# The low halves of the weights: a subtraction on the vector engine, or a negated copy plus an adding DMA

## The chip, the cores and the metric

The kernel runs on one core of a Trainium2 chip. The core has a matrix engine (PE, TensorE; its weight loads are listed apart as PEld), a vector engine (DVE), a scalar engine (ACT), GpSimd (POOL) and a queue engine (SP). POOL and SP here mostly issue DMAs. Each engine runs its own instructions strictly in order and waits on semaphores for the others. The metric is the device time of one execution in microseconds.

## The reference

The reference is a two-layer encoder trunk on 512 tokens of width 1024, all in float32:

```python
for l in range(DEPTH):                       # DEPTH = 2
    x = x + 0.5 * swiglu_ffn(rmsnorm(x, ffn1_norm[l]), ffn1_w_up[l], ffn1_w_down[l])
    x = x + mixer(rmsnorm(x, mix_norm[l]), ...)
    x = x + 0.5 * swiglu_ffn(rmsnorm(x, ffn2_norm[l]), ffn2_w_up[l], ffn2_w_down[l])
    x = rmsnorm(x, final_norm[l])
```

The mixer projects to q, k, v, a gated convolution input and two gates. It runs banded attention in three dilation groups (window 128, 512, 2048 at dilation 1, 4, 16), a depthwise convolution of width 31 with layer norm, combines the two branches by the gates and projects back. The hidden width of the feed-forward part (FFN) is 2816.

## The kernel before

Every weight matrix is read from DRAM once, in pieces of up to 128 x 1024 float32 (512 KB). A matmul here takes operands in the reduced format float32r, so each float32 operand is split in two: an upper half `hi` (the value rounded to float32r) and a lower half `lo` (what is left). `mm3` (L156) then makes three matmuls per product: hi by hi, hi by lo, lo by hi.

The function `stage` (L140) makes one such piece ready. SP loads it into `raw` (2 buffers), ACT copies it, rounding, into `hi` (L152), and DVE subtracts `hi` from `raw` into `lo` (L153). `hi` and `lo` have 4 buffers each, so PE works on one piece while up to three others are made ready. There are 448 pieces. `stage` is called with a priority 150 steps ahead of its place in the program; the order on each engine is set by a scheduler that runs when the program is built.

Who calls it:
- `ffn`: the up projection, 4 pieces for each of 11 pairs of hidden tiles, and the down projection through `proj_cols`. One full piece feeds 24 matmuls of 128x128 by 512 columns.
- `mixer`, in `proj_cols`: the convolution input (`ps_ga`, `ps_gg`), the gates (`ps_gc`, `ps_gA`), and the projections `ps_cp`, `ps_ap`, `ps_o`.
- `mixer`, in `tokens_chunk` (L295): q, k and v, nine chunks per layer. A chunk takes four pieces and goes through all four twice (two token tiles each time, `ps_n`), so that in the second pass a piece feeds 12 matmuls and its buffers come free one after another near the end of the chunk.

In the mixer POOL issues small DMAs: `bias` (L302, two buffers), v tiles to DRAM and back in another order (`vd` L380, `V` L390 to L395), attention results (`od` L463, `sd` L466 to L471) and their return (`oin` L572, `sa` L540). Some of them wait for DVE, ACT or PE. DVE meanwhile runs the convolution (`cv`, L516, 240 instructions per layer) between everything else.

In the last two groups of each down projection and of the output projection (28 pieces in all) the rows are 128 elements (512 bytes) long instead of 256.

Of the kernel before, what the change touches and what calls it, by code (L numbers as in the profile page):

```python
# [11 lines left out]
F32 = mybir.dt.float32  # L12
F32R = mybir.dt.float32r
AF = mybir.ActivationFunctionType
ALU = mybir.AluOpType
# [29 lines left out]
def trunk(ctx: ExitStack, tc: tile.TileContext, A: dict, out: bass.AP):  # L45
    nc = tc.nc
# [89 lines left out]
    def uniq(s):  # L136
        cnt[0] += 1
        return f"{s}_{cnt[0]}"

    def stage(*srcs):  # L140

        a, n1 = srcs[0].shape[1], srcs[0].shape[2]
        n = n1 * len(srcs)
        raw = wp.tile([P, 1024], F32, tag="raw", name=uniq("raw"), bufs=2)
        hi = wp.tile([P, 1024], F32R, tag="hi", name=uniq("hi"))
        lo = wp.tile([P, 1024], F32R, tag="lo", name=uniq("lo"))
        m = a * n
        with tc.high_priority(offset=150):
            rv = raw[:, :m].rearrange("p (a n) -> p a n", a=a)
            for i, src in enumerate(srcs):  # L150
                nc.sync.dma_start(rv[:, :, i * n1:(i + 1) * n1], src)
            nc.scalar.activation(hi[:, :m], raw[:, :m], AF.Copy)  # L152
            nc.vector.tensor_sub(lo[:, :m], raw[:, :m], hi[:, :m].bitcast(F32))  # L153
        return (hi[:, :m].rearrange("p (a n) -> p a n", a=a), lo[:, :m].rearrange("p (a n) -> p a n", a=a))

    def mm3(ps, ah, al, bh, bl, first, last):  # L156
# [61 lines left out]
    def proj_cols(src, c0, rhs, nk, ps):  # L218

        nj = len(ps)  # L220
        step = 8 // nj
        for kk in range(0, nk, step):
            n_ = min(step, nk - kk)
            wh, wl = stage(src[:, kk:kk + n_, c0:c0 + nj * P])
            for j in range(nj):
                for k in range(n_):
                    kg = kk + k
                    mm3(ps[j], wh[:, k, j * P:(j + 1) * P], wl[:, k, j * P:(j + 1) * P], *rhs[kg], kg == 0, kg == nk - 1)


    def ffn(l, w_up, w_down, xg, R, after, deferred=None):
        wu = w_up[l].rearrange("(k p) n -> p k n", p=P)
        wd = w_down[l].rearrange("(k p) n -> p k n", p=P)
        with tc.tile_pool(name=uniq("ffn"), bufs=4) as fp:
            h = []
            for m in range(0, NF, 2):
                pss = {}
                for ab in range(2):
                    pss[ab] = [ps_mm(uniq("ps_a")) if ab == 0 else ps_at(uniq("ps_b")) for _ in range(2)]
                    for kk in range(0, KD, 4):  # L240
                        wh, wl = stage(wu[:, kk:kk + 4, ab * FF + m * P:ab * FF + m * P + 256])
                        for j in range(2):
                            for k in range(4):
                                kg = kk + k
                                mm3(pss[ab][j], wh[:, k, j * P:(j + 1) * P], wl[:, k, j * P:(j + 1) * P], *xg[kg], kg == 0, kg == KD - 1)
                for j in range(2):
                    t = fp.tile([P, S], F32, tag="tmp", name=uniq("t"), bufs=7)
                    nc.vector.tensor_mul(t, pss[0][j], R)
                    nc.scalar.activation(t, t, AF.Silu)
                    nc.vector.tensor_mul(t, pss[1][j], t)  # L250
                    h.append(split(fp, t, "h", 2 * NF))
                if m == 0 and deferred is not None:
                    deferred()
            for ts in ((0, 1), (2, 3), (4, 5), (6,), (7,)):
                pss = [(ps_at if ts[0] in (0, 4, 7) else ps_mm)(uniq("ps_d")) for _ in ts]
                proj_cols(wd, ts[0] * P, h, NF, pss)
                for k, ps in zip(ts, pss):
                    t = fp.tile([P, S], F32, tag="tmp", name=uniq("t"), bufs=7)
                    nc.vector.scalar_tensor_tensor(t, ps, 0.5, R, op0=ALU.mult, op1=ALU.mult)
                    nc.vector.tensor_add(xs[k], xs[k], t)  # L260
                    after(k, fp)


    def mixer(l, xg, R, rr, after):
# [5 lines left out]
        with ExitStack() as mx:  # L270
# [26 lines left out]
            def tokens_chunk(cols):  # L297

                n = S // len(cols)
                bias = mp.tile([P, S], F32, tag="bias", name=uniq("bias"), bufs=2)  # L300
                for i, c0 in enumerate(cols):
                    nc.gpsimd.dma_start(bias[:, i * n:(i + 1) * n], bass.AP(tensor=A["b_in"].tensor, offset=A["b_in"].offset + l * IN_W + c0, ap=[[0, P], [1, n]]))  # L302
                w = [stage(*(win[:, kk:kk + 2, c0:c0 + n] for c0 in cols)) for kk in range(0, KD, 2)]
                for t2 in range(0, TT, 2):
                    ps = [ps_mm(uniq("ps_n")) for _ in range(2)]
                    for k in range(KD):
                        wh, wl = w[k // 2][0][:, k % 2], w[k // 2][1][:, k % 2]
                        xh, xl = xg[k]
                        for t in range(2):
                            ts = slice((t2 + t) * P, (t2 + t + 1) * P)  # L310
                            mm3(ps[t], xh[:, ts], xl[:, ts], wh, wl, k == 0, k == KD - 1)
                    for t in range(2):
                        yield t2 + t, ps[t], bias
# [440 lines left out]
```

## Time and profile before

| | |
|---|---|
| median of 3 runs | 2670.15 us (2669.97 to 2671.66) |
| profiled execution | 2669.43 us, of which the span 2667.5 us |
| PE busy | 2617.8 us, 98% of the span |
| DVE busy | 1599.7 us, 60% |
| ACT busy | 1005.8 us, 38% |
| POOL busy | 110.5 us, 4% |
| mean granted clock of PE | 0.992 |
| moved by DMA | 268.65 MB, mean 101 GB/s |

Busy times are sums of instructions, and a share of the span is an average over stages that differ: DVE is at 60% over all, but full in the attention stages. Matmuls overlap each other, so the time from start to start of two matmuls says more than the length of one.

### The profile page before, as it was taken

What the parts mean: (1) busy time and instruction counts of PE and PEld (TensorE: products, weight loads), DVE (VectorE), ACT (ScalarE), POOL (GpSimd) and SP (SyncE); (2) the same over time, 40 slices, a digit from 0 to 9 for tenths busy, and PEclk for the clock granted to TensorE, in tenths of its full rate; (3) what the DMA queues carried; (4) which work ended last, traced back from release to release, by engine and by line L of the source; (5) the groups of instructions that cost most, each with busy time, mean ns of one, the idle gap of its engine ahead of it and who ended that gap; (6) DMA issues with size and microseconds to landing.
All of it is one profiled execution on the core that took longest, in us unless ns stands there. A gap on an engine that the chain in (4) does not pass through costs nothing.

```text
span 2667.5 us, 30985 instructions
## 1 busy us (share of the span) xinstructions
PE 2617.8 (98%) x12125; PEld 2125.9 (80%) x12125; DVE 1599.7 (60%) x2606; ACT 1005.8 (38%) x1572; POOL 110.5 (4%) x208
## 2 busy tenths in 40 slices
PE   8999999998999999999999999999989999999998
PEld 6888888776877788888888888887767778888887
DVE  4444349999985754443454433599999756444432
ACT  5332232233578242232332322322344963322222
POOL 1000000011011000000000000000011110000000
PEclk9999999999999999999999999999989999999999
DMA  4332333233333333332333322323323343333322
GB/s 155 98 95 91 103 99 105 79 113 97 100 112 110 117 95 96 102 95 95 95 95 95 100 94 93 108 91 114 96 85 121 100 126 103 95 95 96 102 91 75
DMA packets 253778, 268.65 MB, mean 101 GB/s; under 512 B 11624, under 2 KB 238320, under 8 KB 253632
## 3 DMA queue, kind: packets, MB, share of 16 engines
q1 hardware_dynamic: 242112, 234.91, 28.3%
q0 software_dynamic: 11504, 31.76, 4.0%
q8 instruction: 95, 1.56, 0.2%
q14 instruction: 51, 0.42, 0.1%
q10 hardware_dynamic: 16, 0.00, 0.0%
HBM read 251.75 MB, written 14.88 MB: 100 GB/s over the span
## 4 chain that ended last, share of the span: by engine, by line
PE 88%; DVE 7%; ACT 3%; issue 1%; DMA 0%; SPq 0%; ACTq 0%
PE ps_a L158 6%; PE ps_a L159 6%; PE ps_b L157 6%; PE ps_d L157 6%; PE ps_b L158 6%; PE ps_b L159 6%; PE ps_d L159 6%; PE ps_d L158 6%; PE ps_a L157 6%; PE ps_n L158 4%; PE ps_n L157 4%; PE ps_n L159 3%; DVE cv L516 2%; PE ps_cp L158 1%; PE ps_cp L159 1%; PE ps_cp L157 1%
## 5 line engine op out<-in xcount | busy, mean ns | idle before, releaser
L153 DVE TENSOR_TENSOR lo<-raw,hi 128x1024 fp32r<-128x1024 f32 (+1 forms) x448 | 539.2, 1204 | 725.0 <-ACT hi L152 724.0
L152 ACT ACTIVATE hi<-raw 128x1024 fp32r<-128x1024 f32 (+1 forms) x448 | 468.1, 1045 | 1058.3 <-issue 360.2
L516 DVE SCALAR_TENSOR_TENSOR cv<-u,cwc,cv 128x500 f32<-128x500 f32 (+14 forms) x480 | 335.7, 737 | 0.1
L158 PE MATMUL ps_b<-xgl,hi 128*128 128x512 f32 x704 | 275.1, 391 | 0.0
L157 PE MATMUL ps_a<-xgh,hi 128*128 128x512 f32 x704 | 273.5, 389 | 1.1 <-ACT xgh L174 1.1
L159 PE MATMUL ps_a<-xgh,lo 128*128 128x512 f32 x704 | 274.5, 390 | 0.0
L158 PE MATMUL ps_a<-xgl,hi 128*128 128x512 f32 x704 | 274.3, 390 | 0.1
L157 PE MATMUL ps_b<-xgh,hi 128*128 128x512 f32 x704 | 274.0, 389 | 0.0
L159 PE MATMUL ps_b<-xgh,lo 128*128 128x512 f32 x704 | 273.9, 389 | 0.0
L159 PE MATMUL ps_d<-sh,lo 128*128 128x512 f32 x704 | 273.9, 389 | 0.0
L157 PE MATMUL ps_d<-sh,hi 128*128 128x512 f32 x704 | 273.9, 389 | 0.0
L158 PE MATMUL ps_d<-sl,hi 128*128 128x512 f32 x704 | 273.9, 389 | 0.0
L158 PE MATMUL ps_n<-lo,xgh 128*128 128x512 f32 x576 | 228.7, 397 | 3.9 <-DVE lo L153 3.8
L159 PE MATMUL ps_n<-hi,xgl 128*128 128x512 f32 x576 | 225.7, 392 | 0.0
L157 PE MATMUL ps_n<-hi,xgh 128*128 128x512 f32 x576 | 215.8, 395 | 4.7 <-DVE tmp L379 3.4
L157 PEld LDWEIGHTS ps_a<-xgh,hi 128*128 128x128 f32 x704 | 132.0, 188 | 29.0 <-ACT xgh L174 1.5
L158 PEld LDWEIGHTS ps_b<-xgl,hi 128*128 128x128 f32 x704 | 132.2, 188 | 28.0 <-issue 0.7
L159 PEld LDWEIGHTS ps_b<-xgh,lo 128*128 128x128 f32 x704 | 132.2, 188 | 28.0 <-issue 0.7
L158 PEld LDWEIGHTS ps_a<-xgl,hi 128*128 128x128 f32 x704 | 132.2, 188 | 27.9 <-DVE xgl L175 0.5
L159 PEld LDWEIGHTS ps_d<-sh,lo 128*128 128x128 f32 x704 | 132.2, 188 | 27.5
L159 PEld LDWEIGHTS ps_a<-xgh,lo 128*128 128x128 f32 x704 | 132.2, 188 | 27.5 <-issue 0.2
L157 PEld LDWEIGHTS ps_b<-xgh,hi 128*128 128x128 f32 x704 | 132.2, 188 | 27.4
(234 smaller groups left out, 3988.1 us busy)
## 6 DMA issues: line engine op xcount, KB each, us to landing
raw<-in_ffn_w_up_dram SPq DMA_DIRECT2D x176, 512.0 KB, 3.5
raw<-in_w_in_dram SPq DMA_DIRECT2D x88, 512.0 KB, 3.6
raw<-in_ffn_w_down_dram SPq DMA_DIRECT2D x76, 512.0 KB, 3.5
raw<-in_w_in_dram SPq DMA_DIRECT2D x96, 256.0 KB, 3.1
raw<-in_w_conv_proj_dram SPq DMA_DIRECT2D x16, 512.0 KB, 3.5
raw<-in_w_out_dram SPq DMA_DIRECT2D x16, 512.0 KB, 3.5
vd<-tmp POOLq DMA_DIRECT2D x24, 256.0 KB, 2.3
od<-ot POOLq DMA_DIRECT2D x24, 256.0 KB, 3.0
```

Source lines behind the costliest of these rows:

```text
L152: nc.scalar.activation(hi[:, :m], raw[:, :m], AF.Copy)
L153: nc.vector.tensor_sub(lo[:, :m], raw[:, :m], hi[:, :m].bitcast(F32))
L157: nc.tensor.matmul(ps, ah, bh, start=first, stop=False)
L158: nc.tensor.matmul(ps, ah, bl, start=False, stop=False)
L159: nc.tensor.matmul(ps, al, bh, start=False, stop=last)
L516: nc.vector.scalar_tensor_tensor(a[:, t0:t1], u[k][:, t0 + d:t1 + d], cw(l, j, k), a[:, t0:t1], op0=ALU.mult, op1=ALU.add)
```

## The change

`stage` no longer calls DVE. ACT makes `hi` as before and then writes `-hi` into `lo`; POOL issues a DMA that reads the same weights once more from DRAM and adds them to `lo` in place. Each weight is now read from DRAM twice, once into `raw` and once into `lo`. `raw` is read by one instruction (ACT's copy) instead of two. All 448 pieces take the new way; no call names another.

```diff
-    def stage(*srcs):
+    def stage(*srcs, rest="dma"):
...
             nc.scalar.activation(hi[:, :m], raw[:, :m], AF.Copy)
-            nc.vector.tensor_sub(lo[:, :m], raw[:, :m], hi[:, :m].bitcast(F32))
+            if rest == "dma":
+
+                nc.scalar.activation(lo[:, :m], hi[:, :m].bitcast(F32), AF.Copy, scale=-1.0)
+                lv = lo[:, :m].rearrange("p (a n) -> p a n", a=a)
+                for i, src in enumerate(srcs):
+                    nc.gpsimd.dma_start(lv[:, :, i * n1:(i + 1) * n1], src, accum_op=ALU.add)
+            else:
+                nc.vector.tensor_sub(lo[:, :m], raw[:, :m], hi[:, :m].bitcast(F32))
```

In the q and k chunks `srcs` has two parts, so a piece is two DMAs there; elsewhere it is one.

Below the changed lines all line numbers are 7 higher: the accumulating DMA is L158, ACT's negated copy L155, `bias` L309, `vd` L387, `V` L397. DVE loses 448 instructions, ACT gains 445 in all (its table loads fall from 54 to 50, the rest is the negated copies), POOL goes from 161 to 610 rows, SP keeps its order.

ACT, at the pieces of the first v chunk of layer 0 (`hi`, `lo` are the pieces, `sq` the squares of the q and k tiles). Before:

```order
L349 ACTIVATE sq_3451<-z_3449 128x512
L152 ACTIVATE hi_3567<-raw_3566 128x1024
L349 ACTIVATE sq_3511<-z_3509 128x512
L152 ACTIVATE hi_3573<-raw_3572 128x1024
L152 ACTIVATE hi_3579<-raw_3578 128x1024
L349 ACTIVATE sq_3521<-z_3519 128x512
L152 ACTIVATE hi_3585<-raw_3584 128x1024
```

And now:

```order
L356 ACTIVATE sq_3551<-z_3549 128x512
L152 ACTIVATE hi_3667<-raw_3666 128x1024
L356 ACTIVATE sq_3611<-z_3609 128x512
L152 ACTIVATE hi_3674<-raw_3673 128x1024
L155 ACTIVATE lo_3668<-hi_3667 128x1024
L155 ACTIVATE lo_3675<-hi_3674 128x1024
L152 ACTIVATE hi_3681<-raw_3680 128x1024
L152 ACTIVATE hi_3688<-raw_3687 128x1024
L155 ACTIVATE lo_3682<-hi_3681 128x1024
L155 ACTIVATE lo_3689<-hi_3688 128x1024
```

Here the negated copy of a piece stands behind the copy of the next piece; in 431 of the 448 pieces it stands directly behind its own, with none of another piece between.

POOL, from the end of that v chunk into the first q and k chunk of the second dilation group (`vd` stores a v tile, `V` reads it back, `bias` loads the next bias). Before:

```order
L302 DMA bias_4061<-in_b_in_dram 128x256 x2
L380 DMA vd_3563<-tmp_3640 128x512
L380 DMA vd_3563<-tmp_3643 128x512
L390 DMA V_3702<-vd_3563 64x512
L380 DMA vd_3563<-tmp_3696 128x512
L390 DMA V_3705<-vd_3563 128x512
L390 DMA V_3707<-vd_3563 128x512
L380 DMA vd_3563<-tmp_3699 128x512
```

And now:

```order
L387 DMA vd_3663<-tmp_3747 128x512
L397 DMA V_3806<-vd_3663 64x512
L397 DMA V_3809<-vd_3663 128x512
L158 DMA lo_4170<-in_w_in_dram 128x2x256 x2
L387 DMA vd_3663<-tmp_3800 128x512
L158 DMA lo_4179<-in_w_in_dram 128x2x256 x2
L387 DMA vd_3663<-tmp_3803 128x512
L309 DMA bias_4382<-in_b_in_dram 128x256 x2
L397 DMA V_3811<-vd_3663 128x512
L158 DMA lo_4188<-in_w_in_dram 128x2x256 x2
```

The four pieces of the next chunk (`lo_4170` to `lo_4197`) now stand on POOL between and behind DMAs that wait for DVE (`vd`) and for other DMAs (`V`).

On DVE the runs of `cv` between two mask steps of the same attention block were 11, 4, 8, 4 and 8 instructions long in layer 0's second half of the first group; now they are 11, 7 and 9.

## Rows read from the trace of the kernel before

**Rows 1.** The page's first part: span; busy time, share, instructions of each engine.
```profile
span 2667.5 us, 30985 instructions
...
PE 2617.8 (98%) x12125; PEld 2125.9 (80%) x12125; DVE 1599.7 (60%) x2606; ACT 1005.8 (38%) x1572; POOL 110.5 (4%) x208
```

**Rows 2.** The page's chain of work that ended last, shares by engine.
```profile
PE 88%; DVE 7%; ACT 3%; issue 1%; DMA 0%; SPq 0%; ACTq 0%
```

**Rows 3.** Windows: start:end, length, busy us by engine, PEclk, DMA share, GB/s.
```profile
100.00:200.00 100.00, 100.00 (x443) 82.84 (x442) 41.87 (x47) 30.52 (x37) 0.00 (x0) 1.00 0.31 95
650.00:670.00 20.00, 12.43 (x68) 8.57 (x67) 20.00 (x46) 8.53 (x24) 1.84 (x3) 0.63 0.11 29
734.00:867.00 133.00, 130.18 (x702) 101.36 (x701) 89.27 (x206) 107.55 (x204) 19.78 (x37) 1.00 0.35 111
1962.00:1994.00 32.00, 23.23 (x134) 16.31 (x133) 30.86 (x69) 15.97 (x40) 2.38 (x4) 0.73 0.10 26
```

**Rows 4.** Timeline of PE in the FFN: start, length, instruction.
```profile
200.03 0.39 PE L157 MATMUL ps_a<-xgh,hi 128*128 128x512 f32 x1
...
211.59 0.39 PE L157 MATMUL ps_b<-xgh,hi 128*128 128x512 f32 x1
```

**Rows 5.** The page's costliest groups: busy us, mean ns, idle before.
```profile
L153 DVE TENSOR_TENSOR lo<-raw,hi 128x1024 fp32r<-128x1024 f32 (+1 forms) x448 | 539.2, 1204 | 725.0 <-ACT hi L152 724.0
L152 ACT ACTIVATE hi<-raw 128x1024 fp32r<-128x1024 f32 (+1 forms) x448 | 468.1, 1045 | 1058.3 <-issue 360.2
L516 DVE SCALAR_TENSOR_TENSOR cv<-u,cwc,cv 128x500 f32<-128x500 f32 (+14 forms) x480 | 335.7, 737 | 0.1
```

**Rows 6.** The page's DMA queues: packets, MB, share of 16 engines.
```profile
q1 hardware_dynamic: 242112, 234.91, 28.3%
q0 software_dynamic: 11504, 31.76, 4.0%
```

**Rows 7.** The page's DMA issues: count, KB each, median us to landing.
```profile
raw<-in_ffn_w_up_dram SPq DMA_DIRECT2D x176, 512.0 KB, 3.5
...
vd<-tmp POOLq DMA_DIRECT2D x24, 256.0 KB, 2.3
...
V<-vd POOLq DMA_DIRECT2D x14, 256.0 KB, 3.4
```

**Rows 8.** Groups of POOL by line: a DMA of 512 small rows.
```profile
L466 POOL DMA_DIRECT2D sd<-st x4 | 3.0, 762 | 10.4 <-ACT sp L443 10.4
```

**Rows 9.** Timeline of POOL in the token chunks.
```profile
547.60 1.06 POOL L390 DMA_DIRECT2D V<-vd  x2 [1.01 <-DMA vd<-tmp]
```

**Rows 10.** Windows, columns as in rows 3, the stretch of rows 9.
```profile
540.00:548.00 8.00, 7.98 (x44) 6.62 (x43) 8.00 (x12) 2.70 (x4) 2.49 (x5) 1.00 0.79 231
```

**Rows 11.** Waits of the whole span: total us, times, longest us.
```profile
POOL bias L302 <- DVE z L347: 353.0, 10, 96.2
...
ACT hi L152 <- DMA raw<-in_w_in_dram: 83.7, 35, 7.2
...
POOL vd L380 <- DVE tmp L379: 74.9, 15, 16.1
POOL V L392 <- PE ps_pv L454: 74.2, 8, 13.2
```

**Rows 12.** Waits of PE.
```profile
PE ps_n L158 <- DVE lo L153: 3.8, 6, 1.6
```

**Rows 13.** Timeline of the start: POOL's DMAs, PE's first use of a lower half.
```profile
12.61 0.55 POOL L106 DMA_DIRECT2D mask<-in_mask_dram  x1
...
15.47 0.40 PE L159 MATMUL ps_a<-xgh,lo 128*128 128x512 f32 x1
```

**Rows 14.** Timeline of DVE in the first stretch where PE pauses.
```profile
647.92 5.32 DVE L516 SCALAR_TENSOR_TENSOR cv<-u,cwc,cv 128x506 f32<-128x506 f32 x8
...
657.14 5.28 DVE L516 SCALAR_TENSOR_TENSOR cv<-u,cwc,cv 128x500 f32<-128x500 f32 x8
```

**Rows 15.** Windows for line 152 alone: start:end, length, ACT busy, count.
```profile
734.00:867.00 133.00, 19.94 (x19) 1.00 0.35 111
```

## The prediction

> **What bounds the kernel now.** I read the page's engine shares first, then the chain of waits, then busy times by window, then a few stretches of the timeline. PE is busy 2617.8 of 2667.5 us [rows 1] and carries 88% of the chain that ended last [rows 2]. In the FFN nothing else shows: in the window from 100 to 200 us PE is busy for all 100 us at full clock, while DVE has 41.87, ACT 30.52 us and the DMA engines a share of 0.31 [rows 3]. From 200.03 to 211.59 us there are 51 steps from matmul to matmul [rows 4], 0.2267 us each. A full piece of weights feeds 24 matmuls, so PE wants a new one every 24 x 0.2267 = 5.44 us, and with 4 buffers a piece has three pieces' time, 16.3 us, from the freeing of its buffer to its use.
>
> So the most that any change off PE can win is PE's idle time, 2667.5 - 2617.8 = 49.7 us, and the time lost to a low clock behind such pauses. The two largest pauses are in the attention of the first dilation group, one per layer: 7.6 us idle in 650 to 670 at a mean clock of 0.63, and 8.8 us in 1962 to 1994 at 0.73 [rows 3]. DVE is full there; what stands in front of the attention is convolution, in runs of 8 instructions and 5.3 us [rows 14]. PE waits for a lower half itself for only 3.8 us in all [rows 12].
>
> **What the change removes.** 448 subtractions, 539.2 us of DVE [rows 5]. In the FFN, DVE has slack and PE does not wait, so that is worth nothing there. In the token chunks DVE is full, and the removal can end PE's waits for `lo` (3.8 us) and, at most, the two pauses: 7.6 + 8.8 us idle, and clock, (1 - 0.63) x 20 + (1 - 0.73) x 32 = 16.0 us; together 36 us. But the order of the new program still puts runs of 11, 7 and 9 convolution instructions between the mask steps (11, 4, 8, 4, 8 before), so I expect the pauses to stay, and take -4, with bounds of 0 and -36. `raw` comes free one DVE instruction sooner, which shortens ACT's waits for reloads (83.7 us, 35 times [rows 11]); these are inside the latency below.
>
> **What it adds on ACT.** 448 copies of the kind that takes 1.045 us [rows 5], 468 us, so ACT goes to some 1474 of 2667 us. In the FFN this fits. From 734 to 867 us ACT is busy 107.55 of 133 us [rows 3] with 19 pieces in it [rows 15]; 19 more copies make 127.4, or 96%. An in-order engine that full delays something: I take 2 us per layer, 4 in all, with bounds of 0 and 40 (all 20 us on the path in both layers).
>
> **What it adds on DMA.** This is the term on which all hangs. The loads of the weights, queue q1, take 28.3% of 16 engines, 755 us of the span, and the other traffic, q0, 4.0%, 107 us [rows 6]; that is 49.9 ns for a 1-KB packet (0.283 x 2667.5 x 16 / 242112), and 32 packets per engine and piece, 1.6 us. The accumulating DMA moves the same bytes again, but the trace has no accumulating DMA. Bounds from these rows: it costs as much as the plain load (755 us), or each byte goes three times through an engine one after another, source, old value and result (2265 us). I take two plain packets (1510 us): an engine that copies already overlaps its read with its write, and the addition brings one more read. DMA time is then 755 + 1510 + 107 = 2372 us, 89% of the span; in the FFN 1.6 + 3.2 = 4.8 of 5.44 us. It fits, and PE stays the bound there: 0 us. The point from which it decides is (2667.5 - 107 - 755) / 755 = 2.39 plain packets per added packet. Below 1, that the second load makes something faster, I see no way.
>
> The Trainium skill, page "Collectives: The Full Stack", section "The bandwidth ceiling: the fold count and why AG ≠ RS ≠ AR", says that a reduction in the DMA path runs at half the rate of a copy because it needs two source reads, not because the addition costs time. No run here shows it yet; by it the sum is the 2372 us above, without it (the addition costing as a copy) 755 + 755 + 107 = 1617 us.
>
> In 28 pieces the rows are 512 bytes, 64 packets per engine. If a half packet cost as much as a whole one, such a piece would take 64 x (50 + 100) ns = 9.6 us, 4.2 us over PE's 5.44, 116 us in all; if packets scale with bytes, 0. I take 0, since the loads of these pieces hold up nothing now.
>
> **What it adds in latency.** Where a piece has 16.3 us, ACT's two copies, POOL's issue and a landing fit. In the token chunks they have less: in the second pass a piece feeds 12 matmuls, 2.72 us, and the buffer that comes free is wanted three pieces later, 8.16 us. The path of one piece alone: 1.05 + 1.05 on ACT, 0.76 for POOL to issue a DMA of 512 small rows [rows 8], and a landing of 3.5 us for a plain 512 KB [rows 7] plus 1.6 for the second read: 7.96 us. It just fits. But the four pieces share the DMA engines: four additions and the two loads that had no `raw` buffer before make 4 x 3.2 + 2 x 1.6 = 16.0 us of engine time, which can begin when the first copy frees `raw`, 7.1 us before the chunk ends. They end 8.9 us after it, with the tail of a landing (3.5 - 1.6) at 10.8, where 8.16 are there: 2.6 us late. There are 16 such boundaries (9 chunks per layer, 2 layers, without the first of each), 42 us; attention work stands between the chunks in the order of most of them, so I take 25, with bounds of 0 and 75 (if the engines start only when the first addition is issued, 4.7 us at each).
>
> POOL's queue adds to that. Behind each v chunk, in the order shown, the third piece of the next chunk waits behind the last `vd` store, a bias and a `V` that reads it back: two evacuations on DVE at 0.74 [rows 5], 2.3 us of landing [rows 7], four issues at 0.53 [rows 9] are 5.9 us after the chunk's end, and 0.76 + 5.1 more make 11.8, where two pieces' time, 5.44, is there. That is 6.3 us, 3.7 over what is counted above, at the 4 v chunks that another chunk follows 15 us; behind the third v chunk of each layer the gates' pieces stand alike, but have more time. Attention covers some of it, and I take 15 for all six. Below it is 0 at best. Above: POOL's own waits for DVE's v tiles last up to 16.1 us, for PE up to 13.2, for the bias up to 96.2 [rows 11], and nothing was behind them; 6 of 20 us are 120.
>
> The Trainium skill, page "SBUF — State Buffer", section "🔬 SBUF: two separate sides", warns that a DMA issued from GpSimd stalls while DVE holds the port that both share. The trace does not agree for this mix: two issues take 1.06 us [rows 9] in a window where DVE is full [rows 10]. By the rule each addition at the 16 boundaries would be held for one DVE instruction of 0.74 us, 12 us more.
>
> At the start POOL issues some twenty small DMAs before the first addition: the mask at 12.61 ends at 13.16 [rows 13], and 0.76 + 5.1 later, at 19.0, the first `lo` is there, while PE now uses it at 15.47. That is 3.5 us, say 4; bounds of 0 and 10.
>
> **The sum.** -4 + 4 + 0 + 25 + 15 + 4 = +44 us. The profiled execution took 2669.4 us (span 2667.5 and 1.9 around it), 0.7 below the median, so the forecast is 2713 us.
>
> **The rivals.**
> First: the DMA engines become the bound. Over 2.39 plain packets per added packet, every FFN piece waits. At three, 755 + 2265 + 107 = 3127 us of engine time, so about 3130 us, with PE waiting evenly and its clock perhaps lower. For it: nothing here measures the price, and 89% leaves little for jitter. Against it: the only reason for a third pass is that read and write do not overlap, and plain packets do not look like that.
> Second, the other side: DVE's relief dissolves the pauses. DVE has 1.2 us less per piece from 400 us on, the convolution is done sooner, the attention's mask steps are no longer late and the clock does not fall; with PE's waits for `lo` that is 36 us, 2633 us. It decides from the point where a landing at the chunk boundaries stays under 8.16 us, so that nothing eats the gain; the additions must then cost nearly what plain loads cost. For it: DVE is full where PE pauses [rows 3]. Against it: the convolution runs of the new order.
> Third: both small terms cancel, or PE's order hides the boundaries. PE sets the time, 2669 us.
>
> **Chances.** Forecast (DMA fits, boundaries cost) 0.40; DMA-bound 0.28; relief 0.20; cancelled 0.12. This kernel's measurements tell a difference from about 0.2%, 5 us, so faster 0.20, same 0.12, slower 0.68. The range goes from 2640, which leaves out the relief's best cases, to 3130, the DMA bound at three packets; beyond lies about one in ten on each side. The forecast's own range is 2675 to 2790.
>
> **What would show it.** Right: FFN windows with PE full at a DMA share near 0.9; an addition landing in 5 to 6 us; PE's new waits at `ps_n`, for the DMA of `lo`, near chunk ends; POOL waiting for `vd` with additions behind it. Wrong: a DMA share near 1.0 in the FFN and PE waiting for `lo` every 5 us or so (first rival), or a share near 0.6 and pauses gone at 650 and 1970 us (second). The forecast fails first if the price of an added packet is not two plain ones.

## The result: slower by 3.4%

| | before | after |
|---|---|---|
| median | 2670.06 us (2668.8 to 2671.66) | 2759.64 us (2757.56 to 2762.49) |
| ratio, 95% interval | | 1.0336 (1.0318 to 1.0354) |
| profiled execution, its span | 2669.43, 2667.5 us | 2758.02, 2756.1 us |
| PE busy / idle in the span | 2617.8 / 49.7 us | 2644.0 / 112.1 us |
| mean granted clock of PE | 0.992 | 0.978 |

The change costs 89.6 us; 43 were forecast. The span grew by 88.6 us: PE is idle 62.4 us longer, and busy 26.2 us longer with the same matmuls, at a lower mean clock.

Where the program falls behind shows in the start of the first matmul of some stages (us from the start of the span). Between the first `ps_n` and the first `ps_cp` of a layer lie the token chunks, the attention and the gates:

| first matmul of | before | after | later by |
|---|---|---|---|
| `ps_n`, layer 0 | 466.39 | 472.10 | 5.7 |
| `ps_cp`, layer 0 | 857.38 | 899.44 | 42.1 |
| `ps_n`, layer 1 | 1786.61 | 1830.02 | 43.4 |
| `ps_cp`, layer 1 | 2174.68 | 2265.21 | 90.5 |

So 5.7 us are lost before the first chunk, 36.4 and 47.1 us from the chunks through the gates of the two layers, and nothing (-0.6 us) in all the rest.

The page after, in the parts that answer to [rows 1, 2 and 6]: busy times, chain, DMA queues.

```profile
span 2756.1 us, 32357 instructions
PE 2644.0 (96%) x12125; PEld 2146.1 (78%) x12125; DVE 1090.7 (40%) x2158; ACT 1437.9 (52%) x2016; POOL 750.0 (27%) x704
q0 software_dynamic: 251888, 262.48, 59.8%
q1 hardware_dynamic: 242112, 234.91, 26.6%
PE 82%; issue 6%; DMA 5%; ACT 5%; POOL 1%; DVE 0%; SPq 0%; POOLq 0%; ACTq 0%
```

DVE lost 509 us and ACT gained 432, near the 539 and 468 of the costing. The additions, on queue q0 (with POOL's small DMAs, 4.0% before), take more than twice the DMA engines' time of the plain loads on q1.

The new groups (columns as in [rows 5]), and the landings (as in [rows 7]):

```profile
L155 ACT ACTIVATE lo<-hi 128x1024 fp32r<-128x1024 f32 (+1 forms) x448 | 464.8, 1040 | 8.4
L158 POOL DMA_DIRECT2D lo<-in_ffn_w_up_dram x176 | 226.2, 1287 | 728.3 <-ACT lo L155 727.6
...
lo<-in_ffn_w_up_dram POOLq DMA_DIRECT2D x176, 512.0 KB, 6.0
...
lo<-in_w_in_dram POOLq DMA_DIRECT2D x88, 512.0 KB, 7.7
...
lo<-in_w_in_dram POOLq DMA_DIRECT2D x96, 256.0 KB, 8.3
```

A negated copy costs what the first copy costs (1.04 us). An addition takes POOL 1.29 us to issue, where I had 0.76. In the FFN it lands in 6.0 us; for the weights of `w_in` in the mixer in 7.7 and 8.3, the last for half a piece.

Windows of after (columns as in [rows 3]), and then two of them of before:

```profile
0.00:40.00 40.00, 26.54 (x111) 20.71 (x112) 9.82 (x23) 30.57 (x43) 19.49 (x32) 0.91 1.00 250
100.00:200.00 100.00, 100.00 (x443) 82.81 (x442) 19.53 (x29) 49.36 (x57) 23.11 (x18) 1.00 0.96 193
300.00:400.00 100.00, 100.00 (x444) 82.54 (x443) 17.48 (x30) 47.15 (x54) 26.98 (x20) 1.00 1.01 197
640.00:700.00 60.00, 55.12 (x317) 42.50 (x315) 49.47 (x108) 29.48 (x64) 17.27 (x21) 0.97 0.50 120
```
```profile
0.00:40.00 40.00, 29.68 (x136) 23.80 (x137) 17.94 (x30) 25.85 (x38) 11.51 (x26) 1.00 0.58 185
640.00:700.00 60.00, 51.58 (x286) 39.22 (x285) 58.31 (x128) 30.27 (x71) 4.54 (x8) 0.86 0.23 67
```

The FFN (100 to 200 and 300 to 400) is untouched: PE is full at full clock, with the DMA engines at 0.96 and even 1.01. The share adds up the times of packets; above 1 some of them overlap, so it is not a measure of what is left. The start (0 to 40) loses 25 matmuls. The stretch in which PE paused before (650 to 670; in after the same work comes some 25 us later, and 640 to 700 holds both) even became better: 4.9 us idle instead of 8.4, and a clock of 0.97 instead of 0.86.

PE's waits, the group that answers to [rows 12] first (total us, times, longest us):

```profile
PE ps_n L165 <- DMA lo<-in_w_in_dram: 69.5, 19, 8.1
...
PE ps_gc L166 <- DMA lo<-in_w_in_dram: 4.7, 2, 2.5
```

The 3.8 us at `ps_n` became 69.5. The chain of waits through the first boundary between two token chunks shows one of these 19 from inside (start us, us, what):

```profile
489.71 0.24 PE ps_n L166
489.97 1.07 ACT hi L152
491.07 1.07 ACT lo L155
492.14 0.66 issue
492.80 0.70 POOL lo L158
493.52 7.33 DMA lo<-in_w_in_dram
500.85 0.14 issue
500.99 0.77 PE ps_n L165
501.75 0.43 PE ps_n L166
...
505.16 0.29 PE ps_n L166
505.45 0.69 PE ps_n L164 x3
```

PE's own timeline at the same place (start us, us, instruction, idle before and its releaser):

```profile
493.86 0.61 PE L164 MATMUL ps_n<-hi,xgh 128*128 128x512 f32 x2
500.99 0.77 PE L165 MATMUL ps_n<-lo,xgh 128*128 128x512 f32 x1 [6.52 <-DMA lo<-in_w_in_dram]
```

At 489.71 PE runs the last matmul that holds the buffer of the old chunk's first piece. Two copies, the issue and the landing follow, 10.9 us up to 500.85. PE has other work only until 494.47 and stands for 6.52 us. Then it runs at 0.43 us a matmul, the lower clock level (1.2 GHz), until 505.45: ten matmuls in 4.46 us instead of 2.27. So this pause of 6.5 us costs 2.2 more afterwards. In the second of the two windows around it PE is busy for 3.02 of 8 us at a clock of 0.65, POOL issues for 7.13 us and the DMA share is 1.17:

```profile
488.00:496.00 8.00, 6.47 (x29) 5.03 (x27) 8.00 (x16) 6.18 (x8) 3.20 (x4) 1.00 0.40 111
496.00:504.00 8.00, 3.02 (x7) 2.46 (x8) 8.00 (x15) 3.58 (x4) 7.13 (x7) 0.65 1.17 236
```

### The profile page after: what moved, and what is told of

Same layout as the page of the kernel before. It is cut to its first block, busy times and chain, and to the rows that moved or that the text cites. A ratio compares the mean times of both kernels' runs of the same rounds, so it can differ in the third digit from the quotient of the medians.

```text
span 2756.1 us, 32357 instructions
## 1 busy us (share of the span) xinstructions
PE 2644.0 (96%) x12125; PEld 2146.1 (78%) x12125; DVE 1090.7 (40%) x2158; ACT 1437.9 (52%) x2016; POOL 750.0 (27%) x704
## 3 DMA queue, kind: packets, MB, share of 16 engines
q0 software_dynamic: 251888, 262.48, 59.8%
q1 hardware_dynamic: 242112, 234.91, 26.6%
## 4 chain that ended last, share of the span: by engine, by line
PE 82%; issue 6%; DMA 5%; ACT 5%; POOL 1%; DVE 0%; SPq 0%; POOLq 0%; ACTq 0%
PE ps_a L166 6%; PE ps_d L166 6%; PE ps_b L164 6%; PE ps_b L165 6%; PE ps_a L164 6%; PE ps_b L166 6%; PE ps_d L164 6%; PE ps_d L165 6%; PE ps_a L165 6%; DMA lo<-in_w_in_dram 4%; PE ps_n L165 3%; PE ps_n L166 3%; PE ps_n L164 3%; PE ps_cp L165 1%; PE ps_cp L166 1%
## 5 line engine op out<-in xcount | busy, mean ns | idle before, releaser
L155 ACT ACTIVATE lo<-hi 128x1024 fp32r<-128x1024 f32 (+1 forms) x448 | 464.8, 1040 | 8.4
L158 POOL DMA_DIRECT2D lo<-in_ffn_w_up_dram x176 | 226.2, 1287 | 728.3 <-ACT lo L155 727.6
L158 POOL DMA_DIRECT2D lo<-in_w_in_dram x184 | 235.5, 1500 | 477.7 <-ACT lo L155 418.2
L523 DVE SCALAR_TENSOR_TENSOR cv<-u,cwc,cv 128x497 f32<-128x497 f32 (+14 forms) x480 | 331.2, 736 | 0.2
L165 PE MATMUL ps_n<-lo,xgh 128*128 128x512 f32 x576 | 241.4, 420 | 69.5 <-DMA lo<-in_w_in_dram 69.5
L166 PE MATMUL ps_n<-hi,xgl 128*128 128x512 f32 x576 | 238.5, 415 | 0.0
L158 POOL DMA_DIRECT2D lo<-in_ffn_w_down_dram x96 | 128.1, 1334 | 359.0 <-ACT lo L155 359.0
L255 DVE TENSOR_TENSOR t<-ps_a,R 128x512 f32<-128x512 f32 x88 | 60.6, 691 | 342.9 <-PE ps_a L166 318.8
L257 DVE TENSOR_TENSOR t<-ps_b,t 128x512 f32<-128x512 f32 x88 | 60.8, 691 | 338.7 <-PE ps_b L166 338.7
L165 PEld LDWEIGHTS ps_n<-lo,xgh 128*128 128x128 f32 x576 | 115.7, 201 | 100.1 <-issue 38.9
L266 DVE SCALAR_TENSOR_TENSOR t<-ps_d,R 128x512 f32<-128x512 f32 x32 | 22.1, 692 | 378.5 <-PE ps_d L166 378.5
```

The lines of the kernel that those rows point to most:

```text
L155: nc.scalar.activation(lo[:, :m], hi[:, :m].bitcast(F32), AF.Copy, scale=-1.0)
L158: nc.gpsimd.dma_start(lv[:, :, i * n1:(i + 1) * n1], src, accum_op=ALU.add)
L165: nc.tensor.matmul(ps, ah, bl, start=False, stop=False)
L166: nc.tensor.matmul(ps, al, bh, start=False, stop=last)
L523: nc.vector.scalar_tensor_tensor(a[:, t0:t1], u[k][:, t0 + d:t1 + d], cw(l, j, k), a[:, t0:t1], op0=ALU.mult, op1=ALU.add)
```

## The experiments

The theory: the loss arises where buffers come free late, at the boundaries of the token chunks, and not in the mass of the 448 pieces. Its rivals: a cost spread over all pieces; POOL's queue; ACT's second copy. Differences below are to the median of the kernel before in the same comparison (2668.6 to 2670.1 us). In the kernels of the experiments `stage` can work either way, and the edit says which pieces go which way.

**Token chunks back on DVE** (72 pieces; 376 by the adding DMA).

```diff
-                w = [stage(*(win[:, kk:kk + 2, c0:c0 + n] for c0 in cols)) for kk in range(0, KD, 2)]
+                w = [stage(*(win[:, kk:kk + 2, c0:c0 + n] for c0 in cols), rest="dve") for kk in range(0, KD, 2)]
```

> The 72 pieces of the token chunks (q, k, v) are made by the DVE subtraction again, the other 376 keep the addition by DMA. Theory A (the loss sits at the boundaries of the token chunks, where four additions and two reloads come in a burst): the time returns to that of the kernel before, 2670 us, between 2660 and 2680, with the DMA share in the FFN still near 0.95 and PE full there. Rival B (ACT's 448 more copies, or a DMA path that is nearly full everywhere, cost time in all stages): it stays above 2700 us.

Measured: 2697.72 us, ratio 1.0108 (1.0091 to 1.0125), +27.6. Between the two theories: most of the loss is gone, but not all. In its trace most of what is left arises at the start and beside the gates.

**Only the token chunks by the adding DMA** (the reverse: the default is DVE, and the line above says "dma").

> The reverse: only the 72 pieces of the token chunks use the addition by DMA, the other 376 are subtracted on DVE as before. Theory A: nearly the whole loss is there, 2745 to 2765 us. Rival B (the loss is spread over all pieces): a sixth of it, about 2685 us.

Measured: 2743.07 us, ratio 1.0275 (1.0259 to 1.0290), +73. PE's wait in it:

```profile
PE ps_n L165 <- DMA lo<-in_w_in_dram: 79.1, 16, 7.2
```

16 waits for 16 boundaries: 72 of the 448 pieces, 16%, cost 73 us. The rival of an evenly spread cost falls. The two parts add to 100.6 us, more than the 89.6 of both at once; more on this below.

**No detour of v through DRAM.** The v tiles are not stored, and V is read from x instead, so that nothing on POOL waits behind `vd`.

```diff
-                vd = drp.tile([S, AOW], F32, tag="vd", name=uniq("vd"))
+                vd = A["x"][0][:, :AOW]
...
-                    nc.gpsimd.dma_start(vd[tt * P:(tt + 1) * P, :], v)
```

> All pieces by DMA as in the changed kernel; the 24 stores of v tiles (vd) are left out and V is read from the input x instead, so that the result is not that of the reference; POOL has no vd to wait for before an addition. Theory A (burst on the DMA engines): still slower than before by 65 us or more, at 2735 us or above, less some us for 6 MB less traffic. Rival C (POOL's queue: additions stand behind vd stores and V loads that wait): it falls to 2715 us or below.

Measured: 2748.52 us, ratio 1.0294 (1.0279 to 1.0310), +78. POOL's queue behind `vd`, together with the 6 MB of the stores themselves, is 11 of the 89.6 us.

**The second load without the addition**, so `lo` holds the whole weight.

```diff
-                    nc.gpsimd.dma_start(lv[:, :, i * n1:(i + 1) * n1], src, accum_op=ALU.add)
+                    nc.gpsimd.dma_start(lv[:, :, i * n1:(i + 1) * n1], src)
```

> POOL's DMA writes the weights into lo without adding (the lower half is then the whole weight, so the result is not that of the reference); all other instructions are the same. Theory A: a packet costs some 50 to 60 ns instead of 109, the burst at a boundary is 4 x 1.7 + 2 x 1.6 = 10 us instead of 17, and most of the loss goes: 2680 to 2700 us; the DMA share in the FFN falls from 0.95 to about 0.6. Rival C (POOL's queue and the length of the path, not the engines' time): 2735 us or above. Should the packet still cost near 109 ns, then it is not the added read that is dear.

Measured: 2710.23 us, ratio 1.0155 (1.0140 to 1.0170), +40. The queues in the window from 100 to 200 us (packets, MB, share of 16 engines), first of this kernel, then of after:

```profile
q0 software_dynamic: 9732, 9.66, 40.6%
...
```
```profile
q0 software_dynamic: 9859, 9.80, 67.2%
q1 hardware_dynamic: 9504, 9.44, 28.6%
```

1600 us of engine time times the share, over the packets, is 66.7 ns for a copied packet, 109.1 for an added one and 48.1 for a plain load in after. The addition itself thus makes 49 of the 89.6 us; the rest is there without it. These 49 hold three things that fall together: the engines' time, the landing in the FFN (6.0 to 4.2 us) and POOL's issue (1.28 to 0.74 us, medians).

**Half of each token chunk: the second and fourth piece**, and, later, **the first and third**, all else on DVE.

```diff
+ ... rest="dma" if kk % 4 else "dve") for kk in range(0, KD, 2)]      # second and fourth
+ ... rest="dve" if kk % 4 else "dma") for kk in range(0, KD, 2)]      # first and third
```

> Only the second and the fourth piece of each token chunk use the addition by DMA (36 pieces), all others the subtraction on DVE. All four by DMA cost 73 us. Theory A (it is the burst of four additions on the DMA engines at a chunk boundary): with two additions 2 x 3.5 + 2 x 1.6 = 10.2 us of engine time fit into the 15 to 16 us there, and the loss falls far below the half: within 15 us of the time before, 2655 to 2685 us. Rival D (each addition is late by the length of its own path, whatever the others do): about half, 2700 to 2710 us.

Measured: 2691.62 us, ratio 1.0084 (1.0069 to 1.0099), +23: less than half of 73, but above the theory's limit. That sent me back to the order of PE, in the kernel before, at the end of a chunk (`hi_495` and `lo_496` are its first piece, `hi_504` and `lo_505` its fourth, `lo_533` the first of the next):

```
2085 L159 MATMUL ps_n_515_3251<-hi_495_3153,xgl_304_1980 128x512
2086 L157 MATMUL ps_n_515_3251<-hi_498_3160,xgh_327_2159 128x512
...
2103 L159 MATMUL ps_n_515_3251<-hi_504_3174,xgl_388_2550 128x512
2104 L157 MATMUL ps_n_543_3389<-hi_532_3362,xgh_299_1970 128x512
2105 L157 MATMUL ps_n_544_3390<-hi_532_3362,xgh_299_1970 128x512
2106 L158 MATMUL ps_n_543_3389<-lo_533_3363,xgh_299_1970 128x512
```

The last token tile (`ps_n_515`) goes through the four pieces alone, with 6 matmuls each. Between the last use of the first piece and the first use of the next lower half stand 20 matmuls, 20 x 0.2267 = 4.5 us, and not 8.16. So it is at the first three boundaries of each layer; at the other ten boundaries matmuls of the attention stand in between as well. For the second piece there are 26 matmuls, for the third and fourth 45 or more. Hence the second run, which moves the same DMAs and bytes to pieces with less time:

> In the token chunks the first and the third piece of the four by the adding DMA, everything else on DVE as before: the same number of DMAs and bytes as with the second and fourth piece, which cost 23 us. In the order of PE only 21 rows, 20 steps of 0.2267 us, 4.5 us, lie between the last use of a chunk's first piece and the first use of the next chunk's first lower half at the tightest boundaries; the later pieces have more. Theory W, the window of the first piece sets the pause, and the second piece has 6 matmuls, 1.4 us, more: 1.4 us at 16 boundaries, 22 us above, about 2714, 2705 to 2725. Theory D, the DMA engines' burst sets it: the same as the second and fourth, 2685 to 2698.

Measured: 2713.61 us, ratio 1.0161 (1.0144 to 1.0178), +44.5, 21.5 above the other half, as Theory W had it. PE's waits, first of the second and fourth, then of the first and third piece:

```profile
PE ps_n L165 <- DMA lo<-in_w_in_dram: 18.1, 10, 2.8
```
```profile
PE ps_n L165 <- DMA lo<-in_w_in_dram: 44.4, 17, 5.0
```

At equal DMA load the time that a piece has decides. What the other additions do comes on top: with all four pieces the cost rises from 44.5 to 73. In the run of the first and third piece the chain at the first boundary (as above) reads

```profile
483.98 1.07 ACT hi L152
485.08 1.07 ACT lo L155
486.15 0.28 issue
486.43 0.46 POOL lo L158
487.15 5.58 DMA lo<-in_w_in_dram
492.86 0.47 PE ps_n L165
```

which is 8.8 us from the free buffer to the lower half. With all four pieces of the chunks, and these alone, it reads

```profile
485.53 1.07 ACT hi L152
...
487.98 0.43 POOL lo L158
488.70 7.29 DMA lo<-in_w_in_dram
```

which is 10.5 us. POOL's issue is as long in both, the landing 1.7 us longer; 16 times that, an estimate from one boundary, is 27 of the 28.5 us between the two runs.

**ACT's share.** ACT writes `-hi` everywhere, and DVE adds `raw`; there is no second load. Then the same for the token chunks alone and for the gates' pieces alone, and, for comparison, these by the adding DMA. The gates have 32 pieces, not the 64 of the expectations: the run by DMA has 32 DMAs on POOL more than before (240 for 208), and its Rival B comes to 2 us, not 5.

```diff
                 nc.scalar.activation(lo[:, :m], hi[:, :m].bitcast(F32), AF.Copy, scale=-1.0)
...
-                for i, src in enumerate(srcs):
-                    nc.gpsimd.dma_start(lv[:, :, i * n1:(i + 1) * n1], src, accum_op=ALU.add)
+                nc.vector.tensor_add(lo[:, :m], raw[:, :m], lo[:, :m].bitcast(F32))
```

> ACT writes the negated copy in all 448 pieces as in the changed kernel, but DVE adds raw to it; no second load. This has ACT's whole load and DVE's whole load, without the added DMA traffic and without POOL. Theory E (ACT's copies are what costs in the gates, the DMA burst what costs in the token chunks): PE loses time from 740 to 880 us and from 2080 to 2200 us, 15 to 25 us, and little in the token chunks: 2685 to 2695 us. Rival F (in the gates too it is the DMA path): 2670 to 2675 us. Rival G (ACT's copies cost in the token chunks as well): above 2700 us.

> The 72 pieces of the token chunks get ACT's negated copy, and DVE adds raw to it; no second load, all other pieces as before. The same 72 pieces with the adding DMA cost 73 us. Theory A, the burst of additions and reloads on the DMA engines is the cost: 2670 to 2690 us, and no pauses of 5 us or more at the chunk boundaries. Theory B, the second instruction on ACT is the cost: 2720 us or more, with the same pauses.

> Only the 64 pieces of the two gates use the DMA, the other 384 the DVE. Theory E: some 20 us slower than before, 2685 to 2695 us, with PE waiting for ACT (the exponentials) and for lo at ps_gc from 740 to 880 us. Rival B: 27.6 x 64 / 376 = 5 us, 2675 us.

> The 64 pieces of the gates get ACT's negated copy, and DVE adds raw to it; no second load, all other pieces as before. The same 64 pieces with the adding DMA cost 30 us. Theory A, ACT is full there and its copies are the cost: 2690 to 2700 us, PE waiting for ACT's exponentials (sp) as with the DMA. Theory B, the DMA's landing is the cost: 2670 to 2680 us, and the wait for sp is gone.

Measured: everywhere 2700.45 us, ratio 1.0119 (1.0104 to 1.0134), +32; token chunks 2674.09, 1.0019 (1.0010 to 1.0028), +5; gates by DMA 2698.60, 1.0111 (1.0096 to 1.0126), +30; gates by ACT and DVE 2677.29, 1.0032 (1.0020 to 1.0044), +8. In the token chunks ACT's second copy alone, with no DMA behind it, costs 5 of 73 us; on the path of the first piece it is still 1.07 of the 10.5 us. In the gates it is 8 of 30. The windows from 742 to 880 us of before, of the gates by ACT, and of the gates by DMA:

```profile
742.00:880.00 138.00, 135.18 (x710) 104.21 (x708) 92.81 (x207) 106.59 (x197) 22.46 (x42) 1.00 0.36 114
```
```profile
742.00:880.00 138.00, 132.40 (x698) 101.93 (x696) 89.76 (x207) 117.80 (x208) 20.56 (x39) 1.00 0.35 108
```
```profile
742.00:880.00 138.00, 131.05 (x671) 100.17 (x670) 62.24 (x169) 115.12 (x206) 36.83 (x49) 0.97 0.67 150
```

PE's wait for the mask step `sp` in the run of the gates by ACT (11.8 us in 8 waits before):

```profile
PE ps_T L451 <- ACT sp L448: 17.4, 16, 3.0
```

Against the first theory of the last run the copies are not most of the 30 us; against its second, PE still waits for `sp` with them. PE loses 2.8 us of busy time to the copies, and 1.4 more to the DMA; but with the DMA the clock falls to 0.97 too, and 27 matmuls fewer are done. The 32 us of the copies everywhere are more than 5 and 8. By the starts of the stages they too arise from the chunks through the gates (13.6 and 17.2 us in the two layers, against 0.9 and 10.0 in the two runs together), and PE then waits longer for `lo` at `ps_n` than the 3.8 us of before; why there is more of it than in the two runs together is not shown.

```profile
PE ps_n L164 <- DVE lo L157: 15.5, 11, 2.5
```

**Token chunks and gates on DVE** (344 pieces by the adding DMA; the expectations count 312 and 300, by the same slip), and then **the first 12 pieces of the program too** (332).

```diff
+                proj_cols(win, 3 * AW + 3 * D + c * 256, xg, KD, ps, rest="dve")
+                proj_cols(win, 3 * AW + 2 * D + c * 256, xg, KD, ps, rest="dve")
...
+ ... rest="dve" if l == 0 and w_up is A["ffn1_w_up"] and m < 6 else "dma")
```

> The pieces of the token chunks and of the two gates (72 + 64) are subtracted on DVE, the other 312 use the DMA. With the token chunks alone on DVE 27.6 us were left. Theory E (5 us of these at the start, the rest in the gates beside the last attention group, where ACT is full): about 2675 us, 2668 to 2682. Rival B (a loss that goes with the number of pieces): 27.6 x 312 / 376 = 23 us, 2693 us.

> 300 of the 448 pieces by the adding DMA: the token chunks and the gates keep DVE's subtraction, and so do the first 12 pieces of the program. With those 12 by DMA the kernel took 2682.7 us, 14 more than before. Theory A, the start is most of those 14: 2668 to 2677 us, and PE's first use of a lower half at 15 to 16 us as before. Theory B, the 300 other pieces cost something everywhere: 2679 us or more, with PE's start as before.

Measured: 2682.69 us, ratio 1.0055 (1.0038 to 1.0072), +14; and 2670.83, 1.0004 (0.9995 to 1.0014), +2, no difference. The windows of the latter:

```profile
0.00:40.00 40.00, 29.63 (x130) 23.79 (x131) 16.82 (x29) 25.97 (x38) 11.59 (x26) 1.00 0.59 185
100.00:200.00 100.00, 100.00 (x443) 82.84 (x442) 19.38 (x28) 48.17 (x55) 23.27 (x19) 1.00 0.94 191
```

So three quarters of the pieces take the adding DMA for nothing, with the DMA engines at 0.94, and all of the loss comes with the pieces of three places: 73 us with the token chunks and 30 with the gates, each measured alone, and 12 with the start, the difference of the last two runs. They sum to 115, not 89.6, so they partly cover each other. By the starts of the stages that is from the chunks through the gates: 73.6 us there with the chunks alone, 26.1 with the gates alone, 83.5 with both; why the gates cost only 10 beside the chunks is not shown. Nor are the 12 us all at the start: the run without DVE there is 6.1 us late at the first `ps_n`, the run with it 1.5, and 3.7 us more of the former come between the first `ps_cp` of layer 0 and the next layer, where both kernels do the same. No version beats the kernel before.

## Why the prediction was right in sign and short in size

**FFN and projections, 0 us: right.** The forecast was an added packet at two plain ones, 2372 us of DMA time in all. Measured over the span: 59.8% and 26.6%, together 2381 us; less 107 us of other traffic on q0 the additions took 1541 us, 2.04 times the 755 of the plain loads before. In the FFN's window an added packet cost more, 109.1 / 48.1 = 2.27, at a DMA share of 0.96, and PE was full. The reason given for the price, that reading and writing overlap, no run shows; without the addition a copy on POOL's queue already costs 66.7 / 48.1 = 1.39. Nor need 2.39 be the point at which it decides, since the share passed 1 with PE full. The 28 pieces with short rows, put at 0, take the DMA in the last run too, and cost nothing. The rule of the Trainium skill, page "Collectives: The Full Stack", section "The bandwidth ceiling: the fold count and why AG ≠ RS ≠ AR" (in collectives a reduction moves at half the rate of a copy), gives 2 where these runs give 2.27 against the plain load on SP's queue and 109.1 / 66.7 = 1.64 against a copy that POOL issues.

**The first rival** (DMA engines as the bound, 3130 us) needed three packets and did not come. **The third** (PE's order hides the boundaries) fell with the 69.5 us of waits.

**The chunk boundaries, 25 us: the step that failed.** Alone they cost 73 us, near the upper bound of 75. I wrote that in the second pass a piece feeds 12 matmuls and that its successor is wanted 8.16 us after it comes free. In the order of the kernel before, one tile passes alone, and at the six tightest boundaries the time is 4.5 us; I had counted loops in the code and not rows of the order. The path of the first piece was put at 7.96 us for itself; it took 10.9, since I had put the issue and the landing (7.33, not 3.5 + 1.6) too short; these 7.33 hold the issue of the piece's second half, which the sum left out. 10.9 - 4.5 = 6.4 is the pause of 6.52 us. Third, I priced no clock behind a new pause, although [rows 3] show the clock of 0.63 at the old ones: 2.2 us for this pause, and at most 26.2 of the 88.6 us over the span. The Trainium skill, page "TensorE: Matmul & The Clock Gate", section "🔬 Part 1: The HAM clock gate (the "warmup" mystery)", has 426.7 ns from start to start of 512 columns at the lower level; the trace agrees with 0.43 us.

**POOL's queue, 15 us: right in size**, 11 by the run without the detour, the stores included. The waits before the bias, which the upper bound named, did not come: POOL stood for 353 us before these loads, and in after it never does, since additions now stand in front of them.

**ACT, 4 us: too small, and the wrong thing.** The copies cost 8 us in the gates alone, 5 in the token chunks and 32 everywhere, within the bounds of 0 and 40. But I wrote that the gates' pieces have more time for the landing; by DMA the same pieces cost 22 us more, a term that the sum put at nothing.

**The start, 4 us: near in size, by another mechanism.** PE is 5.7 us late at the first `ps_n`. POOL's queue of small DMAs is as read, with the first addition issued at 13.24 behind the mask; it lands 6.8 us later, at 20.0, where 19.0 was forecast. But PE does not wait for it. Its timeline in after (start us, us, instruction, idle before and its releaser) shows the transposes of x in front:

```profile
19.13 1.12 PE L624 MATMUL ps_x<-ident,xnat 128*128 128x128 f32 x4 [3.25 <-ACT x L626]
20.04 1.92 PE L216 MATMUL ps_bc<-dg,ones 128*128 128x512 f32 x2
21.75 2.52 PE L624 MATMUL ps_x<-ident,xnat 128*128 128x128 f32 x12
24.03 0.47 PE L166 MATMUL ps_a<-xgh,lo 128*128 128x512 f32 x1
```

PE uses its first lower half at 24.03 instead of 15.47, because the new order puts it there, and before that it stands for 3.25 us until ACT has copied `x`. 25 matmuls fewer by 40 us are the 5.7 us. That the forecast came near is luck.

**The second rival, DVE's relief, -4 us:** perhaps. From 640 to 700 us PE's idle time fell by 3.5 us and the clock rose by 0.11, 6.6 us of 60, and PE's wait for `sp` there (5.3 us) is gone. But PE also comes there some 25 us later, which gives DVE time for the mask steps, and in another order; no run separates these. It was more than paid for at the boundaries, before and behind.

## What to carry to other kernels

When a change lengthens the path from a free buffer to its next use, read the time that is there from the rows of the engine's order between the two uses, at the worst place, not from an average or from the loops; the average here had room for everything, and 72 of 448 pieces made most of the loss. A transfer that is free at a steady rate can be dear where several start at once: here they also landed later. Add to each new pause of the matrix engine the time at the lower clock behind it.

## What the runs showed of the hardware that I had not expected

- An addition into on-chip memory costs POOL about as much to issue for half a piece as for a whole one: 1.28 us for a whole piece (median in the FFN), 2.43 us for the two halves of the first piece in the chain above. Without the addition a whole piece takes 0.74 us.
- A DMA that POOL issues into the reduced format costs the DMA engines 66.7 ns a packet even without the addition, against 48.1 for the plain load into float32 on SP's queue; whether queue or format makes the difference no run shows.
- The DMA engines hold a share of 0.94 to 1.01 over 100 us without PE waiting once.
